# Stick-breaking attention summed by parts: scanned products times differences of neighbouring values

## The chip, the cores and the metric

The kernel runs on one core of one Trainium2 chip. The time is device microseconds from one launch to its end. The kernel before took 1382.73 us (median of three runs, 1382.43 to 1384.61).

## The reference, cut to what matters

The program is one decoder layer on 1024 tokens of width 1024: a mixer with two head groups (SSD and stick-breaking attention, eight heads of 64 each), cross-attention to 256 memory tokens, a squared-ReLU MLP, and norms. Only the stick-breaking attention is changed:

```python
def stick_breaking_attention(q, k, v):
    """q,k,v (B,H,S,Dh). A[t,s] = sigmoid(z_ts) * prod_{s<j<t} (1 - sigmoid(z_tj)), s < t strictly."""
    ...
    for i in range(s_len // Q_BLOCK):
        ...
        logits = jnp.einsum("bhqd,bhkd->bhqk", qb, kb) * scale
        ...
        log_stay = jnp.where(mask, jax.nn.log_sigmoid(-logits), 0.0)
        log_beta = jax.nn.log_sigmoid(logits)
        later = lax.cumsum(log_stay, axis=3, reverse=True) - log_stay
        w = jnp.where(mask, jnp.exp(log_beta + later), 0.0)
        outs.append(jnp.einsum("bhqk,bhkd->bhqd", w, vb))
```

For a row t, let R[s] be the product of the staying probabilities 1 - sigmoid(z) over s <= j < t, with R[t] = 1. The weight of position s is sigmoid(z_ts) R[s+1], which is also R[s+1] - R[s].

## The kernel before, in words

All float32 operands of a matmul are split into a high part (rounded by ScalarE) and a low part (the rest, by VectorE); a product is three matmuls (`mm3`), or two where one side's parts are stacked. The helper `split` (L104 and L107 in the profile: `act` and `tt`) makes both parts. `stt` is L114. The order of each engine's queue is fixed when the program is built: instructions go in the order in which they are traced, those under `later(by)` ahead (negative) or behind (positive), as far as their operands and buffers are expected to be there. `interleave` traces two streams side by side.

Early part, up to about 236 us: the input projections and the SSD heads. `proj_v(0)` makes the values of heads 0 to 3, `proj_qk(0)` and `proj_qk(1)` queries and keys of heads 0 to 3; they are traced beside `ssd`, which loads VectorE and ScalarE. `proj_v` takes eight token tiles of 128 in turn: 24 matmuls into a PSUM tile `vps` of 128 by 256 (`mm_ps`: three buffers `m0` and one `m1` in the early part; `qk_ps`: the three `m0` in the later one), ScalarE writes the high part into a tile `vst`, VectorE the low part, and SP's queue stores both to `vd` in DRAM (L573).

Attention, from about 250 to 516 us: eight heads, the first seven beside the rest of the projections (`proj_qk(2)`, `proj_v(1)`, `proj_qk(3)`, the memory's keys and values), the last beside the first part of the output projection. Per head the POOL queue loads values (`vt`), queries (`qs`) and keys (`kk`). Rows of queries go in eight blocks i of 128, with W = 128 (i + 1) columns. For each: matmuls `z` (L723); ScalarE's sigmoid of minus z into `stay` and of z into `beta` (L104); POOL sets one column behind the row to 0 (L717); VectorE scans `stay` from right to left (L727), so that it holds the products R; VectorE multiplies `beta` by `stay` shifted by one column (L107). Blocks go in pairs m; for a pair, TensorE transposes the rows of `beta` in 128 by 128 pieces (`wT`, L745), the result is split (`wTh` and `wTl`, `wlast` for the piece on the diagonal), and matmuls with the values sum into `ops` (L759). After every second pair the two halves of `ops` are added into `oT`. `beta` and `stay` have two narrow and two wide buffers each.

The scan runs with multiply and add, its second operand `dg1` being zeros with an identity in the last 128 columns, so that it starts at 1 on the diagonal:

```python
nc.vector.tensor_tensor_scan(out=stay[:, 0:W][:, ::-1], data0=stay[:, 0:W][:, ::-1],
                             data1=B.dg1[:, S - W:S][:, ::-1], initial=0.0,
                             op0=ALU.mult, op1=ALU.add)
tt(beta[:, 0:W], beta[:, 0:W], stay[:, 1:W + 1], ALU.mult)
```

Of the kernel before, what the change touches and what calls it, by code (L numbers as in the profile page):

```python
# [76 lines left out]
# columns of the packed per-partition constants  # L77
C_GMIX, C_GSSD, C_GSB, C_CW, C_CB, C_GMEM, C_GXA, NCOLS = 0, 8, 12, 16, 40, 46, 54, 62
# pieces of the packed weights, in the order of their use
# [11 lines left out]
def hybrid_trunk(ctx: ExitStack, tc: tile.TileContext, xT, x, cols, rows, gain, fing, wzd, wp, out):  # L91
# [39 lines left out]
    @contextmanager  # L131
    def later(by):
        """what is traced here gives way on its engine to what is traced up to `by` instructions after it"""
        tc.cur_priority += by
        yield
        tc.cur_priority -= by

# [10 lines left out]
                            fill=0.0, base=0, channel_multiplier=-1)  # L148
    nhalf = cp.tile([P, NT], F32, name="nhalf")
# [9 lines left out]
    # the first use of the scalar engine's functions, before any data is there  # L159
# [15 lines left out]
    def staging():  # L175
        """a tile that weights are loaded to: one in three from the pool of a phase that has room for it"""
        nst_[0] += 1
        if third and nst_[0] % 3 == 0:
            return third[0].tile([P, 528], F32, tag="wst3", bufs=1, name="wst")
        return wr.tile([P, 528], F32, tag="wst", bufs=2, name="wst")  # L180
# [26 lines left out]
    def wsl(ws, k, lo, n, width=256):  # L207
        """columns lo..lo+n of row block k in a chunk cut into pieces of several row blocks"""
        per = 512 // width if width != 264 else 2
        h, l = ws[k // per]  # L210
        o = (k % per) * width + lo
        return h[:, o:o + n], l[:, o:o + n]
# [11 lines left out]
    def interleave(a, b, total_a, total_b, need=None):  # L224
        """trace two streams side by side: each yields the share of its work that it has just traced;
        b may also yield ("need", x), which traces a up to x first"""
        da = db = 0.0
        a, b = iter(a), iter(b)
        live_a = live_b = True
        while live_a or live_b:  # L230
            if live_a and (not live_b or da / total_a <= db / total_b):
                v = next(a, None)
                live_a = v is not None
                da += v or 0.0
                continue
            v = next(b, None)
            if v is None:
                live_b = False
            elif isinstance(v, tuple):
                while live_a and da < v[1]:  # L240
                    w = next(a, None)
                    live_a = w is not None
                    da += w or 0.0
            else:
                db += v

    def rows_T(hn):
        """128 by 512 -> [128 columns, 4, 128 rows], in PSUM"""
# [6 lines left out]
    qd = dp.tile([8, P, S], F32, name="qd")  # L255
    kd = dp.tile([8, 192, S], F32, name="kd")
    vd = dp.tile([S, 8, P], F32, name="vd")
    rd = dp.tile([64, P], F32, name="rd")
# [6 lines left out]
    # =================== phase A: input projection and SSD ===================  # L265
# [23 lines left out]
    def load_x(k):  # L289
        """a block of xT: times the gain, split"""  # L290
# [19 lines left out]
    # the tensor engine's clock rises once it has been busy for some microseconds: products that nothing reads,  # L310
    # while the first loads are under way
# [26 lines left out]
    def conv_block(fb, ps2):  # L338
        """fb: 0..3 xs, 4 B, 5 C"""
# [37 lines left out]
    # factors of the stick-breaking logits' rows  # L377
    rq = [cp.tile([P, NT], F32, name=f"rq{i}") for i in range(2)]
    for r, f in zip(rq, (0.125, -0.125)):
        ts(r, rtok, f, None, ALU.mult)  # L380
# [12 lines left out]
    # token-major projections: z (with dt), v  # L393
# [32 lines left out]
    # a = -exp(a_log) = -sigmoid(a_log) / sigmoid(-a_log)  # L426
# [53 lines left out]
    def decay(c):  # L480
        """exp of minus the sums of a * dt between a chunk's tokens, 1 before the row's own"""
# [28 lines left out]
    def ssd():  # L510
      state = None
      for c in range(NT):
# [44 lines left out]
        # gate, sums of squares for the norm  # L557
# [6 lines left out]
    def proj_v(ch, p, ps_fn):  # L564
        ws = pieces(f"v{ch}", 0, 4)
        for t in range(NT):
            ps = tok_proj(ws, t, 256, 256, "vps", ps_fn)
            pv = ps[:, :256].rearrange("p (h d) -> p h d", h=4)
            vt = p.tile([P, 512], F32R, tag="qh", bufs=2, name="vst").rearrange("p (h c) -> p h c", h=4)
            with later(-EV):  # L570
                act(vt[:, :, 0:64], pv, scale=rtok[:, t:t + 1])
                stt(vt[:, :, 64:128], pv, rtok[:, t:t + 1], vt[:, :, 0:64].bitcast(F32), ALU.mult, ALU.subtract)
            nc.sync.dma_start(out=vd[t * P:(t + 1) * P, 4 * ch:4 * ch + 4, :], in_=vt.bitcast(F32))  # L573
            yield 1.0
# [77 lines left out]
    def need(h):  # L652
        """the share of the streams beside it that a head waits for"""
# [9 lines left out]
    # =================== phase B: stick-breaking attention ===================  # L663
    oT = big(1, [P, 4, S], F32, "oT")

    class Bufs:
        """the tiles that attention works in"""

        # narrow and wide rows: so many from the start, so many once the projection's operands are gone
        ROWS = {"beta": {True: 2, False: 2}, "stay": {True: 2, False: 2}}  # L670

        def __init__(self, ctx):
# [3 lines left out]
            nc.gpsimd.tensor_copy(out=self.dg1[:, S - P:S], in_=ident)  # L676
            self.wlast = [[p.tile([P, 512], F32R, name=f"wlast{a}{b}") for b in range(2)] for a in range(1)]
            for a in self.wlast:
                for b in a:
                    nc.gpsimd.memset(b[:, 256:384].bitcast(F32), 0.0)  # L680
# [15 lines left out]
    def attention(heads, B, need=lambda h: 0):  # L696
        for h in heads:
# [3 lines left out]
            nc.gpsimd.dma_start(out=vt, in_=vd.rearrange("(t p) h c -> p t (h c)", p=P)[:, :, P * h:P * h + P])  # L701
            qs = B.t("qs", [P, S], 2)
# [9 lines left out]
            for m in range(4):  # L712
                wb = []
                for i in (2 * m, 2 * m + 1):
                    W = P * (i + 1)
                    beta, stay = B.row("beta", W), B.row("stay", W)
                    nc.gpsimd.memset(stay[:, W:W + 1], 0.0)  # L717
                    for off in range(0, W, 512):
# [3 lines left out]
                        for a in range(2):  # L722
                            nc.tensor.matmul(out=z[:, 0:nn], lhsT=qs[:, i * P:(i + 1) * P],  # L723
                                             rhs=ks[a][off // 512][:, 0:nn], start=a == 0, stop=a == 1)
                        act(stay[:, off:off + n], z[:, 0:n], AF.Sigmoid, scale=rq[1][:, i:i + 1])
                        act(beta[:, off:off + n], z[:, 0:n], AF.Sigmoid, scale=rq[0][:, i:i + 1])
                    nc.vector.tensor_tensor_scan(out=stay[:, 0:W][:, ::-1], data0=stay[:, 0:W][:, ::-1],  # L727
                                                 data1=B.dg1[:, S - W:S][:, ::-1], initial=0.0,
                                                 op0=ALU.mult, op1=ALU.add)
                    tt(beta[:, 0:W], beta[:, 0:W], stay[:, 1:W + 1], ALU.mult)  # L730
                    wb.append(beta)
# [4 lines left out]
                for s2_ in range(m + 1):  # L736
# [19 lines left out]
                    for sb in range(2):  # L756
                        v = vt[:, 2 * s2_ + sb, :]
# [3 lines left out]
                if m % 2 == 1:  # L761
                    od = oT[64 * hh:64 * hh + 64, h // 2, 512 * (m // 2):512 * (m // 2) + 512]
                    act(od, ops[64:128, :])
                    tt(od, ops[0:64, :], od, ALU.add)
# [17 lines left out]
    def load_h(n, t, after=None):  # L782
        """not before `after` is written: what is needed sooner has the queues till then"""
# [13 lines left out]
    # output projection, by the heads of the first kind  # L797
# [44 lines left out]
    # =================== phase C: output projection, cross-attention ===================  # L842
# [30 lines left out]
    def turn(t):  # L873
        """rows of h, transposed and split"""
# [36 lines left out]
    # the row factors go into the softmax  # L911
# [18 lines left out]
    # softmax over the memory, values  # L930
# [49 lines left out]
    # the first half's normed rows are needed until its last projections: their places are taken after them  # L980
# [31 lines left out]
    # the products of the MLP go by blocks of two by two in seven products (Winograd's form):  # L1012
    # S1 = A21 + A22, S2 = S1 - A11, S3 = A11 - A21, S4 = A12 - S2
    # T1 = B12 - B11, T2 = B22 - T1, T3 = B22 - B12, T4 = T2 - B21
    # P1 = A11 B11, P2 = A12 B21, P3 = S4 B22, P4 = A22 T4, P5 = S1 T1, P6 = S2 T2, P7 = S3 T3
    # C11 = P1 + P2, U2 = P1 + P6, U3 = U2 + P7, C12 = U2 + P5 + P3, C21 = U3 - P4, C22 = U3 + P5
# [16 lines left out]
    def norm_rows(t):  # L1033
        """rows of h, normed: two tiles of 512 columns"""
# [20 lines left out]
    def normB(t):  # L1055
        """the normed rows, transposed: the right-hand operands of the first product, 128 tokens of them"""
# [49 lines left out]
    # =================== phase D: squared-ReLU MLP, final norm ===================  # L1106
    def prod(ps, a, b):
        """one of the seven products: a of two tiles [128, 4 * 128], b one of B"""
# [33 lines left out]
    # the left-hand operands of the second product's seven, in DRAM  # L1142
# [75 lines left out]
    def prod2(q, ops, accumulate, tail=False):  # L1218
        """a product of a group: four blocks of tokens, accumulated over the group's pairs"""
# [26 lines left out]
    def squares(t, c, n, st=None):  # L1246
        """sums of squares of half a row block"""
# [5 lines left out]
    def gained(t, c, n, eng, gfin):  # L1253
        """times the final gain: out of place, as the squares are of what comes in"""
# [19 lines left out]
    for g in range(NG):  # L1274
        Bm = []

        def load(j):
# [7 lines left out]
            # B11, B12, B21, B22  # L1285
# [56 lines left out]
def _layout(inp):  # L1342
# [5 lines left out]
    def cut(w, rows_per, n0, n1, k0=0, k1=None):  # L1348
        """columns n0..n1 of w: rows in blocks of 128, rows_per blocks side by side in a piece"""
# [53 lines left out]
```

## Time and profile before

| | us |
|---|---|
| median of three runs (lowest, highest) | 1382.73 (1382.43, 1384.61) |
| span of the profiled execution | 1381.4 |
| TensorE, VectorE, ScalarE busy in the span | 1318.0, 1002.7, 721.8 |
| of 141 to 236 us (95.0): TensorE, VectorE, ScalarE | 95.0, 66.2, 41.5 |
| of 236 to 516 us (280.0): TensorE, VectorE, ScalarE | 259.0, 237.1, 191.8 |

Of the profiled execution only the span is given, from its first to its last instruction; the median of the runs is 1.3 us above it. An engine's busy time is the time that its instructions cover. Matmuls are pipelined and their ends are modelled, so a busy TensorE need not be at its peak. PEld is the load of weights into TensorE, which overlaps matmuls. A wait is put down to what released it last. The granted TensorE clock has a mean of 0.992 of full speed over the span.

### The profile page before, as it was taken

The numbers are of one execution on the slowest core, as the hardware profiler recorded it, in microseconds if no ns is written. First come the engines' busy times: TensorE is split into PE (matmuls) and PEld (weight loads), VectorE is DVE, ScalarE is ACT, GpSimd is POOL, SyncE is SP. The second block draws the span as 40 slices with busy tenths as digits, with TensorE's granted clock in tenths as the row PEclk, the third lists the DMA queues.
The fourth block names the chain that finished last, engine by engine and source line by source line (L and its number), as shares of the span: only waits on it lengthen the run. The fifth ranks groups of instructions, "written<-read, shape, count | busy, mean of one in ns | idle before, by whom it ended". The sixth has DMA issues, their size and how long they took to land.

```text
span 1381.4 us, 18631 instructions
## 1 busy us (share of the span) xinstructions
PE 1318.0 (95%) x6469; PEld 1064.5 (77%) x6469; DVE 1002.7 (73%) x1570; ACT 721.8 (52%) x1384; POOL 234.8 (17%) x293
## 2 busy tenths in 40 slices
PE   9999999999988999999898999999999999999886
PEld 7989977787766778887676888888887888888765
DVE  7748864688999875638789666666559855677896
ACT  7355642667777653626555544554444544444343
POOL 0000002111101110000263323321331000000543
PEclk9999999999999999999998999999999999999999
DMA  6111355854567224111224445444368933633242
GB/s 215 39 62 49 125 157 137 229 145 138 142 196 204 70 79 127 47 31 31 92 77 151 163 156 163 134 141 153 130 210 297 317 112 93 234 92 98 71 127 86
DMA packets 102878, 183.79 MB, mean 133 GB/s; under 512 B 9664, under 2 KB 20992, under 8 KB 102784
## 3 DMA queue, kind: packets, MB, share of 16 engines
q1 hardware_dynamic: 85168, 158.14, 36.2%
q0 software_dynamic: 15664, 18.88, 5.4%
q10 hardware_dynamic: 1952, 5.58, 1.2%
q8 instruction: 51, 0.84, 0.2%
q14 instruction: 43, 0.35, 0.1%
HBM read 128.00 MB, written 54.56 MB: 132 GB/s over the span
## 4 chain that ended last, share of the span: by engine, by line
PE 74%; DVE 15%; ACT 4%; issue 3%; DMA 2%; POOL 1%; SPq 0%; DVEq 0%; POOLq 0%; ACTq 0%
PE P L203 7%; PE P L205 7%; PE P L204 7%; PE pr L203 6%; PE pr L204 6%; PE pr L205 6%; DVE stay L727 4%; DVE wlo L107 3%; PE qkps L203 2%; PE o L205 2%; PE qkps L204 2%; PE qkps L205 2%; PE o L204 2%; PE o L203 2%; PE ops L759 2%
## 5 line engine op out<-in xcount | busy, mean ns | idle before, releaser
L204 PE MATMUL pr<-wlo,whi 128*128 128x512 f32 x448 | 177.7, 397 | 10.9 <-DVE wlo L107 10.7
L203 PE MATMUL pr<-whi 128*128 128x512 f32 x448 | 176.8, 397 | 0.7 <-ACT whi L104 0.7
L205 PE MATMUL pr<-whi,wlo 128*128 128x512 f32 x448 | 177.2, 395 | 0.0
L107 POOL TENSOR_TENSOR c<-c 128x512 f32<-128x512 f32 x64 | 88.9, 1400 | 247.9 <-ACT c L104 224.3
L204 PEld LDWEIGHTS pr<-wlo,whi 128*128 128x128 f32 x448 | 84.4, 188 | 34.8 <-DVE wlo L107 15.3
L107 DVE TENSOR_TENSOR wlo<-w1r,whi 128x512 fp32r<-128x512 f32 x92 | 78.2, 851 | 41.8 <-ACT whi L104 41.5
L104 ACT ACTIVATE whi<-w1r 128x512 fp32r<-128x512 f32 x92 | 58.1, 632 | 94.6 <-PE P L204 70.0
L203 PE MATMUL P<-T,whi 128*128 128x512 f32 x256 | 101.7, 397 | 1.9 <-ACT T L104 1.9
L205 PE MATMUL P<-T,wlo 128*128 128x512 f32 x256 | 101.5, 396 | 0.0
L204 PE MATMUL P<-T,whi 128*128 128x512 f32 x256 | 101.1, 395 | 0.0
L203 PEld LDWEIGHTS pr<-whi 128*128 128x128 f32 x448 | 84.3, 188 | 21.3 <-ACT whi L104 1.4
L205 PEld LDWEIGHTS pr<-whi,wlo 128*128 128x128 f32 x448 | 84.4, 188 | 19.8
L104 ACT ACTIVATE c<-c 128x512 f32<-128x512 f32 x128 | 78.7, 628 | 26.1 <-DVE c L107 24.7
L727 DVE TENSOR_TENSOR_SCAN stay<-stay,dg 128x128 f32<-128x128 f32 (+3 forms) x64 | 85.0, 1346 | 6.6 <-ACT stay L104 6.2
L104 ACT ACTIVATE whi<-wst 128x512 fp32r<-128x512 f32 (+1 forms) x88 | 54.5, 628 | 58.6 <-PE o L205 16.6
L104 ACT ACTIVATE whi<-us 128x512 fp32r<-128x512 f32 x64 | 40.3, 629 | 83.0 <-PE pr L204 73.8
L203 PE MATMUL P<-B,whi 128*128 128x512 f32 x192 | 76.9, 401 | 0.0
L204 PE MATMUL P<-B,whi 128*128 128x512 f32 x192 | 76.6, 399 | 0.0
L205 PE MATMUL P<-B,wlo 128*128 128x512 f32 x192 | 76.5, 398 | 0.0
L107 DVE TENSOR_TENSOR wlo<-wst,whi 128x512 fp32r<-128x512 f32 (+1 forms) x88 | 61.1, 706 | 21.0 <-ACT whi L104 20.4
L107 DVE TENSOR_TENSOR wlo<-pair,whi 128x512 fp32r<-128x512 f32 x96 | 74.3, 774 | 0.0
L107 DVE TENSOR_TENSOR wlo<-us,whi 128x512 fp32r<-128x512 f32 x64 | 47.6, 744 | 36.3 <-ACT whi L104 36.0
(327 smaller groups left out, 3515.1 us busy)
## 6 DMA issues: line engine op xcount, KB each, us to landing
ud<-c SPq DMA_DIRECT2D x112, 256.0 KB, 2.7
wst<-in_wp SPq DMA_DIRECT2D x104, 256.0 KB, 2.8
w1r<-in_wp SPq DMA_DIRECT2D x16, 1024.0 KB, 6.4
us<-ud SPq DMA_DIRECT2D x64, 256.0 KB, 2.6
pair<-in_wp SPq DMA_DIRECT2D x16, 1024.0 KB, 6.7
kk<-kd POOLq DMA_DIRECT2D x32, 256.0 KB, 5.5
p<-ud SPq DMA_DIRECT2D x24, 256.0 KB, 2.6
u<-ud SPq DMA_DIRECT2D x24, 256.0 KB, 2.7
```

Of the source, the lines that this page charges most:

```text
L104: nc.scalar.activation(out=out, in_=in_, func=func, **kw)
L107: (eng or nc.vector).tensor_tensor(out=out, in0=a, in1=b, op=op)
L203: nc.tensor.matmul(out=ps, lhsT=a[0], rhs=b[0], start=start, stop=False)
L204: nc.tensor.matmul(out=ps, lhsT=a[0], rhs=b[1], start=False, stop=False)
L205: nc.tensor.matmul(out=ps, lhsT=a[1], rhs=b[0], start=False, stop=stop)
L727: nc.vector.tensor_tensor_scan(out=stay[:, 0:W][:, ::-1], data0=stay[:, 0:W][:, ::-1], data1=B.dg1[:, S - W:S][:, ::-1], initial=0.0, op0= ...
L759: nc.tensor.matmul(out=ops[:, oc:oc + 256], lhsT=v, rhs=w[:, sb * 256:sb * 256 + 256], start=(s2_ == 0 and sb == 0 and j == 0), stop=(last ...
```

## The change

Summed by parts, the output of a row t is v[t-1] minus the sum over s < t of R[s] (v[s] - v[s-1]), with v[-1] = 0. So the scanned products R go into the transposes and the matmuls directly, `beta` and its product are not formed, and `proj_v` stores differences of neighbouring values in place of values. From the diagonal on, R is 1: the scan takes the maximum with a triangle `tri` in place of adding an identity. The term v[t-1] comes out of the last block of a pair, where the weights to the right of the diagonal are 1: there a second set `vl` (stored in `ve`) is used, whose rows are the plain values less the neighbour (the last row without its own), and the sign is turned where `ops` is read.

Rows must be moved down by one partition to form the differences. `proj_v` collects two tiles in `vt`, and three transfers on SP's queue write the shifted copy `vb`: the last row of the pair before, the last row of the first tile, and 127 rows of both tiles at once. VectorE forms `vl` and `vb`, and three splits and three stores follow in place of two. The new tiles `vb` and `vl` share the tag `ql` (two buffers) with the low parts of `proj_qk`, the split results the tag `qh` (two buffers).

```diff
     def proj_v(ch, p, ps_fn):
         ws = pieces(f"v{ch}", 0, 4)
+        prev = None
         for t in range(NT):
             ps = tok_proj(ws, t, 256, 256, "vps", ps_fn)
-            pv = ps[:, :256].rearrange("p (h d) -> p h d", h=4)
-            vt = p.tile([P, 512], F32R, tag="qh", bufs=2, name="vst").rearrange("p (h c) -> p h c", h=4)
+            odd = t % 2
+            if not odd:
+                vt = p.tile([P, 2, 256], F32, tag="vv", bufs=2, name="vv")
             with later(-EV):
-                act(vt[:, :, 0:64], pv, scale=rtok[:, t:t + 1])
-                stt(vt[:, :, 64:128], pv, rtok[:, t:t + 1], vt[:, :, 0:64].bitcast(F32), ALU.mult, ALU.subtract)
-            nc.sync.dma_start(out=vd[t * P:(t + 1) * P, 4 * ch:4 * ch + 4, :], in_=vt.bitcast(F32))
+                act(vt[:, odd], ps[:, :256], scale=rtok[:, t:t + 1])
+            if odd:
+                vb = p.tile([P, 2, 256], F32, tag="ql", bufs=2, name="vb")
+                if prev is None:
+                    nc.gpsimd.memset(vb[0:1, 0], 0.0)
+                else:
+                    nc.sync.dma_start(out=vb[0:1, 0], in_=prev[P - 1:P, 1])
+                nc.sync.dma_start(out=vb[0:1, 1], in_=vt[P - 1:P, 0])
+                nc.sync.dma_start(out=vb[1:P], in_=vt[0:P - 1])
+                vl = p.tile([P, 512], F32, tag="ql", bufs=2, name="vl")[:, :256]
+                stt(vl, vt[:, 1], notlast, vb[:, 1], ALU.mult, ALU.subtract)
+                tt(vb, vt, vb, ALU.subtract)
+                for j, src in enumerate((vb[:, 0], vb[:, 1], vl)):
+                    o = p.tile([P, 4, P], F32R, tag="qh", bufs=2, name="vst")
+                    with later(-EV):
+                        split(o[:, :, 0:64], o[:, :, 64:128], src.rearrange("p (h d) -> p h d", h=4))
+                    dst = ve[t // 2] if j == 2 else vd[(t - 1 + j) * P:(t + j) * P]
+                    nc.sync.dma_start(out=dst[:, 4 * ch:4 * ch + 4, :], in_=o.bitcast(F32))
+                prev = vt
             yield 1.0
...
-        ROWS = {"beta": {True: 2, False: 2}, "stay": {True: 2, False: 2}}
+        ROWS = {"stay": {True: 2, False: 3}}
...
-            nc.gpsimd.tensor_copy(out=self.dg1[:, S - P:S], in_=ident)
+            nc.gpsimd.tensor_copy(out=self.dg1[:, S - P:S], in_=tri)
...
-                for b in a:
-                    nc.gpsimd.memset(b[:, 256:384].bitcast(F32), 0.0)
+                for b, v in zip(a, (1.0, 0.0)):
+                    nc.gpsimd.memset(b[:, 256:384].bitcast(F32), v)
...
+            vl = B.t("vl", [P, 4, P], 2)
+            nc.gpsimd.dma_start(out=vl, in_=ve.rearrange("t p h c -> p t (h c)")[:, :, P * h:P * h + P])
...
-                    beta, stay = B.row("beta", W), B.row("stay", W)
-                    nc.gpsimd.memset(stay[:, W:W + 1], 0.0)
+                    stay = B.row("stay", W)
...
-                        act(stay[:, off:off + n], z[:, 0:n], AF.Sigmoid, scale=rq[1][:, i:i + 1])
-                        act(beta[:, off:off + n], z[:, 0:n], AF.Sigmoid, scale=rq[0][:, i:i + 1])
+                        act(stay[:, off:off + n], z[:, 0:n], AF.Sigmoid, scale=rq[:, i:i + 1])
...
-                                                 op0=ALU.mult, op1=ALU.add)
-                    tt(beta[:, 0:W], beta[:, 0:W], stay[:, 1:W + 1], ALU.mult)
-                    wb.append(beta)
+                                                 op0=ALU.mult, op1=ALU.max)
+                    wb.append(stay)
...
-                        v = vt[:, 2 * s2_ + sb, :]
+                        v = vl[:, m, :] if last and sb == 1 else vt[:, 2 * s2_ + sb, :]
...
-                    act(od, ops[64:128, :])
-                    tt(od, ops[0:64, :], od, ALU.add)
+                    act(od, ops[64:128, :], scale=-1.0)
+                    tt(od, od, ops[0:64, :], ALU.subtract)
```

`notlast` is a column of ones with a 0 in the last row; `rq` keeps the factor -0.125 alone.

## Rows read from the trace of the kernel before

**Rows 1.** The page: span; each engine's busy time, share, instructions
```profile
span 1381.4 us, 18631 instructions
...
PE 1318.0 (95%) x6469; PEld 1064.5 (77%) x6469; DVE 1002.7 (73%) x1570; ACT 721.8 (52%) x1384; POOL 234.8 (17%) x293
```

**Rows 2.** Each engine's busy time in two stretches of the span
```profile
core 0: us, PE busy (x) PEld busy (x) DVE busy (x) ACT busy (x) POOL busy (x), PEclk, DMA share, GB/s
141.00:236.00 95.00, 95.00 (x546) 78.25 (x545) 66.20 (x123) 41.47 (x93) 3.10 (x4) 1.00 0.48 135
236.00:516.00 280.00, 258.96 (x1456) 203.54 (x1455) 237.06 (x350) 191.75 (x408) 40.96 (x132) 0.99 0.55 152
```

**Rows 3.** The chain that ended last, 236 to 516 us, shares by line
```profile
by line: DVE stay L727 21.2%; PE ops L759 7.7%; issue 7.4%; DVE beta L107 6.8%; DMA wst<-in_wp 5.0%; ACT stay L104 5.0%; PE wT L745 4.3%; DVE wTl L107 4.2%; ACT beta L104 4.2%; PE z L723 2.9%; ACT whi L104 2.7%; PE qkps L204 2.7%; PE qkps L
```

**Rows 4.** VectorE groups, 236 to 516 us: busy us, mean ns | idle before
```profile
L727 DVE TENSOR_TENSOR_SCAN stay<-stay,dg 128x128 f32<-128x128 f32 (+3 forms) x64 | 85.0, 1346 | 6.6 <-ACT stay L104 6.2
L107 DVE TENSOR_TENSOR beta<-beta,stay 128x128 f32<-128x128 f32 (+3 forms) x64 | 47.6, 750 | 9.4 <-PE z L723 5.4 <-ACT beta L104 2.3 <-POOL h L785 0.8
L107 DVE TENSOR_TENSOR wlo<-wst,whi 128x512 fp32r<-128x512 f32 x32 | 21.7, 685 | 6.0 <-ACT whi L104 5.7
```

**Rows 5.** ScalarE groups by shape, 236 to 516 us
```profile
L104 ACT ACTIVATE beta<-z,rq 128x512 f32<-128x512 f32 x48 | 33.3, 693 | 7.3 <-PE wT L745 7.1
L104 ACT ACTIVATE beta<-z,rq 128x384 f32<-128x384 f32 x16 | 9.3, 581 | 3.4 <-PE wT L745 3.4
L104 ACT ACTIVATE beta<-z,rq 128x256 f32<-128x256 f32 x16 | 7.6, 475 | 0.0
L104 ACT ACTIVATE beta<-z,rq 128x128 f32<-128x128 f32 x16 | 6.3, 393 | 0.0
```

**Rows 6.** Tile vst, 140 to 236 us: ns min/median/max, first and last start
```profile
L104 ACT ACTIVATE vst<-vps,rtok x8: 453/472/476, 145.0 to 173.0; 128x256 fp32r<-128x256 f32 x8
L114 DVE SCALAR_TENSOR_TENSOR vst<-vps,rtok,vst x8: 475/479/484, 145.8 to 173.7; 128x256 fp32r<-128x256 f32 x8
L573 SPq DMA_DIRECT2D vd<-vst x8: 319/320/407, 146.3 to 174.2; - x8
```

**Rows 7.** The same tile, 236 to 516 us
```profile
L104 ACT ACTIVATE vst<-vps,rtok x8: 467/477/497, 266.3 to 324.1; 128x256 fp32r<-128x256 f32 x8
```

**Rows 8.** Groups on tiles of 128x256 by shape, 236 to 516 us
```profile
L107 DVE TENSOR_TENSOR wlast<-wT,wlast 128x256 fp32r<-128x256 f32 x32 | 13.3, 415 | 1.0 <-ACT wlast L104 1.0
L104 ACT ACTIVATE wlast<-wT 128x256 fp32r<-128x256 f32 x32 | 12.2, 381 | 2.0 <-PE wT L745 2.0
```

**Rows 9.** DMA, whole run: packets, MB, share; issues, KB each, us to landing
```profile
q1 hardware_dynamic: 85168, 158.14, 36.2%
...
vd<-vst SPq DMA_DIRECT2D x16, 256.0 KB, 2.0
...
kd<-qh SPq DMA_DIRECT2D x32, 128.0 KB, 3.1
```

**Rows 10.** TensorE in order of time: start us, us; two short stretches
```profile
309.27 0.28 PE L203 MATMUL vps<-whi,xh 128*128 128x256 f32 x1
309.39 0.28 PE L204 MATMUL vps<-wlo,xh 128*128 128x256 f32 x1
...
354.05 0.39 PE L203 MATMUL qkps<-xh,whi 128*128 128x512 f32 x1
354.28 0.39 PE L204 MATMUL qkps<-xl,whi 128*128 128x512 f32 x1
```

**Rows 11.** Waits, 236 to 516 us: us in total, times, longest us
```profile
POOL stay L717 <- DVE beta L107: 125.0, 40, 8.7
POOL kk L710 <- PE z L723: 28.4, 7, 5.5
ACT beta L104 <- PE wT L745: 10.5, 10, 2.4
ACT whi L104 <- DMA wst<-in_wp: 9.9, 10, 3.3
```

More of the change, by code (lines that the diff above doesn't have):

```diff
@@ L148, in hybrid_trunk @@
                             fill=0.0, base=0, channel_multiplier=-1)
+    notlast = cp.tile([P, 1], F32, name="notlast")
+    nc.gpsimd.tensor_scalar(out=notlast, in0=ident[:, P - 1:P], scalar1=-1.0, scalar2=1.0, op0=ALU.mult, op1=ALU.add)
     nhalf = cp.tile([P, NT], F32, name="nhalf")
@@ L257, in hybrid_trunk @@
     vd = dp.tile([S, 8, P], F32, name="vd")
+    ve = dp.tile([4, P, 8, P], F32, name="ve")
     rd = dp.tile([64, P], F32, name="rd")
@@ L376, in hybrid_trunk @@
     rtok = rstd_of(cp, sps[:, :NT], NT, D, "rtok")
-    rq = [cp.tile([P, NT], F32, name=f"rq{i}") for i in range(2)]
-    for r, f in zip(rq, (0.125, -0.125)):
-        ts(r, rtok, f, None, ALU.mult)
+    rq = cp.tile([P, NT], F32, name="rq")
+    ts(rq, rtok, -0.125, None, ALU.mult)
     rbc = xp.tile([P, S], F32, name="rbc")
```

## The prediction, made before the change was run

> **What bounds the kernel now.** I read the page's first part, then the stretches, then the chain of waits inside the one that matters, then its costliest groups. TensorE is recorded busy for 95% of a span of 1381.4 us [rows 1]. The change touches only 141 to 516 us: the value projections of the early part (beside the SSD part) and the attention. From 141 to 236 us TensorE's records leave no idle time at all; from 236 to 516 us they leave 280.0 - 259.0 = 21 us, VectorE is busy 237 us of the 280 and ScalarE 192 [rows 2]. Matmul records overlap: neighbours start 0.12 us apart at 256 columns and 0.23 us at 512, while each is recorded as 0.28 and 0.39 us long [rows 10]. So recorded idle time is the least that TensorE has to spare, not the most. The chain through this stretch runs over VectorE more than over anything else: the scans hold 21.2%, the product `beta` 6.8%, the second sigmoid 4.2% [rows 3]. That is where the change cuts.
>
> **What goes.** The 64 products leave VectorE: 47.6 us [rows 4]. The 96 second sigmoids leave ScalarE: 33.3 + 9.3 + 7.6 + 6.3 = 56.5 us [rows 5]. The 64 one-column memsets leave the POOL queue, where they stood 125.0 us waiting for products, with the loads of keys behind them [rows 11]; I book nothing for that, because those loads then wait for their buffers (28.4 us in the same rows) and no matmul is named as waiting for one. Of the chain the removed steps hold 6.8 + 4.2 = 11.0% of 280 us = 31 us. The least that they give back is less than TensorE's idle 21 us, if another wait is next. What is late next is the scan, which stays, and the buffers: a row is now held through its transposes, as `beta` was (ScalarE waited 10.5 us for that [rows 11]), with three wide buffers in place of two and two. I take the middle of 21 and 31: **26 us saved**, with 10 and 31 as ends.
>
> **What stays at the same price.** The scan's second operation becomes a maximum and its second operand a triangle. No row shows a scan with a maximum; the nearest is the scan itself, 1346 ns in the mean [rows 4], and I take that. A scan that got one more pass would cost at most the removed products again, 47.6 us; nothing speaks for it. The transposes, splits, value matmuls and the two operations on `oT` keep their number and shapes. One more load per head (256 KB, eight in all) goes to the POOL queue that has lost its memsets. The change of `rq`, the constant `notlast` and the fills of `wlast` are single small instructions: nothing.
>
> **What is added.** For each pair of token tiles in `proj_v`, four pairs in each of two projections: three transfers from SBUF to SBUF that move the rows down by one, on SP's queue; one scalar_tensor_tensor; one subtraction of 128x512; three splits where there were two; three stores where there were two. In engine time this is little. VectorE per pair: 0.48 + 0.69 + 3 x 0.42 less 2 x 0.48 = 1.5 us; ScalarE one 0.47 us evacuation kept per tile plus 3 x 0.38 = 1.1 us more [rows 4, 6, 8]. Over four pairs that is 6 us and 5 us beside work that leaves 29 us of VectorE idle early and, after the removal, some 85 us idle later: nothing on the path.
>
> **The shift is the doubtful price.** It moves 127 rows of 2 KB (254 KB) and everything else of the pair waits for it. From below: the store of `vst`, 128 rows and 256 KB, lands in 2.0 us [rows 9]. From above: all 127 rows one after the other. SP's queue moved 85168 packets in 36.2% of 16 engines' 1381.4 us, which is 94 ns a packet [rows 9]; 127 of them take 11.9 us. Of the store's 2.0 us its eight packets an engine are 0.75, so 1.25 is fixed; together **13.2 us**. Every listed transfer has 64 or 128 rows, and 16 equal shares exist for them; 127 rows have no equal shares but single rows. I take the upper end, and keep the lower as a rival.
>
> The Trainium skill, DMA: Bandwidth & Descriptors, section "Why a DMA increments its semaphore by 16 and not by 1", says that a transfer gets the largest number of engines up to 16 that divides the outermost count on both sides, and names 127 partitions as a case that gets one. No run here shows it. By that rule the shift has the upper price and the sum below; by the nearest row, 2.0 us, the sum would be the second rival's.
>
> **What waits for it.** `vb` and `vl` take turns in two buffers of one tag (`ql`), so a pair's shift can't start before the pair ahead is split. A pair then takes 13.2 + 0.6 of issue (two single-row transfers go ahead of it at 0.32 each [rows 6]) + 0.48 + 0.69 + about 1.8 for the overlapped splits = 16.8 us. VectorE, ScalarE and SP each work in a fixed order, so behind the waiting subtraction stand the SSD part's VectorE work (early) and the scans and splits of attention (later); behind the waiting stores on SP stand the next weight pieces.
>
> Early projection: its eight evacuations start from 145.0 to 173.0 us, 4 us a tile [rows 6]. With the first pair complete at about 149.5, four pairs in file end at 149.5 + 4 x 16.8 = 216.7, where the last store now starts at 174.2: 42 us late. TensorE can run ahead by the four PSUM tiles that `mm_ps` has: 4 x 24 matmuls x 0.23 = 22 us [rows 10]. So **20 us lost**, with 5 (other work fits in between) and 42 as ends. TensorE has no idle time here to take it up [rows 2].
>
> Later projection: evacuations from 266.3 to 324.1 us, 16.5 us a pair [rows 7], which is nearly the serial pace already, so no queue builds up. What remains is four waits of 13.2 - 2.0 = 11.2 us on VectorE and ScalarE. TensorE can run ahead by three PSUM tiles of 24 x 0.12 = 2.9 us, 8.6 us at best, so between 4 x 2.6 = 10 and 45 us; I take **20 us lost**, nearer to the covered end, since the attention's own matmuls also go on for a while. The lower end is 0, if VectorE's new 85 us of idle time happen to lie there.
>
> **Sum.** 1381.4 - 26 + 20 + 20 = 1395.4 us for the profiled execution. Only its span is given; the median of the runs, 1382.73, is 1.3 above it, so **1397 us**. The case's own range is 1384 to 1422 (relief 21 with losses of 30 and 30 at the top).
>
> **Rivals.**
> First, the shift is slow and hidden: the subtraction stands late enough in VectorE's and ScalarE's order that other work fills the 13 us, and only the buffers cost something. For it: VectorE loses 47.6 us of work; the later pace is the serial one [rows 7]. Against it: TensorE has no spare time from 141 to 236 us. 1381.4 - 26 + 8 + 4 + 1.3 = 1369 us.
> Second, the shift is spread over the engines like the store of `vst` [rows 9]: it lands in 2 to 4 us and a pair takes under 8 us, its pace of today. For it: the nearest row. Against it: 127 rows. Then 1381.4 - 26 + 1.3 = 1357 us.
> Third, no change: the scan with its held buffers takes the place of the product, so the relief is 10 us, and a half-hidden shift gives 11 back: 1383 us. For it: the scans hold three times the product's share of the chain [rows 3].
> The first two end on the other side from the forecast, and the point at which the sign turns is clear: losses in `proj_v` of 26 us in all, 3.3 us for each of eight shifts.
>
> **Chances.** Forecast 0.50, first rival 0.26, second 0.14, third 0.10. The sizes are rough, so some of each case spills over. Faster by over 0.2%: 0.06 of the forecast, 0.20 of the first, all 0.14 of the second, 0.02 of the third = 0.42. Within 0.2% (2.8 us, about what a measurement of this kernel can tell from no change): 0.04 + 0.03 + 0.04 = 0.11. Slower: 0.40 + 0.03 + 0.04 = 0.47. Cases of both signs hold much of the chance, so the range has to reach from the second rival, 1357, to the top of the forecast's, 1422.
>
> **What would show it.** In the profile after: the median time to landing of `vb` from `vt` near 13 us (forecast, first rival) or near 2 (second). The evacuations of the early projection ending near 200 us in place of 173, and TensorE idle between 150 and 236 us where it had none, with VectorE's subtraction named behind a transfer. The stretch that holds attention, 280 us now [rows 2], being shorter by some 26 us would show the relief, with `beta` gone and VectorE near 195 us busy in it. The prediction is wrong if the shift lands in a few microseconds, if TensorE stays gapless through the early stretch, or if the relief is far above 31 us, which would say that TensorE's hidden reserve (overlapped records [rows 10]) was the larger part.

## The result, and the profile after

| | us |
|---|---|
| before, median of four runs beside the changed kernel | 1383.65 |
| after, median of four runs (lowest, highest) | 1467.91 (1465.84, 1471.80) |
| after / before, 95% interval | 1.0606 [1.0585, 1.0627] |
| span of the profiled execution after | 1467.2 |

The change made the kernel 84 us slower, 46 us above the top of the predicted range. The first lines of the page after answer to [rows 1]. In its second part each digit is the busy share of one of 40 slices of 36.7 us; PEclk is the granted clock in tenths.

```profile
span 1467.2 us, 18461 instructions
...
PE 1331.6 (91%) x6469; PEld 1078.6 (74%) x6469; DVE 973.1 (66%) x1529; ACT 686.3 (47%) x1312; POOL 237.4 (16%) x240
...
PE   8999757996459989999988899999999999999987
...
PEclk9999878998869999999999899999999999999999
```

In all VectorE lost 30 us and ScalarE 35.5 us of work, and TensorE has the same number of matmuls. TensorE has two dips that it didn't have before, around the fifth to seventh and the tenth to twelfth slice: those are the two runs of `proj_v`. The stretches that answer to [rows 2] hold about the same matmuls, so they are longer here (busy time of each engine, granted clock); the last two rows are 20 us from inside each dip.

```profile
core 0: us, PE busy (x) PEld busy (x) DVE busy (x) ACT busy (x) POOL busy (x), PEclk, DMA share, GB/s
141.00:282.00 141.00, 108.51 (x554) 87.31 (x553) 70.45 (x135) 44.85 (x106) 5.79 (x9) 0.85 0.37 109
282.00:600.00 318.00, 256.32 (x1436) 206.07 (x1435) 201.15 (x297) 153.68 (x326) 38.96 (x73) 0.92 0.55 151
...
200.00:220.00 20.00, 11.20 (x40) 8.65 (x41) 6.03 (x12) 1.77 (x4) 0.00 (x0) 0.66 0.34 106
...
420.00:440.00 20.00, 9.94 (x42) 7.83 (x42) 6.24 (x15) 4.49 (x12) 0.92 (x1) 0.68 0.31 101
```

The early stretch went from 95 us without a gap to 141 us with 32 us of idle TensorE, the later one from 280 to 318 us with 62 us idle. What stops TensorE is in the waits of 141 to 600 us (us in total, times, longest):

```profile
DVE vl L114 <- DMA vb<-vv: 85.0, 8, 12.8
...
ACT vst L104 <- DVE vb L107: 50.5, 4, 15.4
...
PEld wT L769 <- DVE stay L752: 32.3, 35, 13.8
...
PE yp L538 <- DVE seg L107: 25.8, 3, 10.7
PE wT L769 <- DVE stay L752: 25.7, 26, 13.6
...
PEld yp L538 <- DVE seg L107: 20.0, 2, 11.2
PE ops L783 <- DVE wlast L107: 19.9, 2, 10.1
...
PE ops L783 <- DVE wTl L107: 10.4, 2, 10.2
```

Read from top to bottom it is one story: eight times VectorE waits for the shifted copy, 10.6 us each; ScalarE's splits wait for VectorE; and TensorE waits for things that have nothing to do with `proj_v` (SSD's `seg`, attention's `stay`), because VectorE makes them after the instruction on which it stands. Of TensorE's 94 us of idle time in the two stretches, 82 end with something of VectorE's (the four lines of PE: 25.8 + 25.7 + 19.9 + 10.4). In order of time (start, length; in brackets the idle time before and its releaser):

```profile
151.46 0.72 SPq L588 DMA_DIRECT2D vb<-vv  x1
...
154.61 0.68 DVE L107 TENSOR_TENSOR wb<-xstok,rowt 128x512 f32<-128x512 f32 x1
165.09 0.48 DVE L114 SCALAR_TENSOR_TENSOR vl<-vv,notlast,vb 128x256 f32<-128x256 f32 x1 [9.79 <-DMA vb<-vv]
...
169.82 1.97 PE L538 MATMUL yp<-wa,seg 128*128 128x64 f32 x8 [8.61 <-DVE seg L107]
...
351.37 0.58 PE L783 MATMUL ops<-wTl,vt 128*128 128x256 f32 x1 [10.23 <-DVE wTl L107]
```

The first shift is issued at 151.46 us and used at 165.09: 13.6 us. The eight take 13.6 to 17.7 us, 14.7 in the mean. VectorE stops at 155.3 us (154.61 + 0.68), TensorE at 161.2 (169.82 - 8.61): it ran ahead by 5.9 us, not 22, then stood for 8.6 us before `yp`, SSD's matmul on a product that VectorE had yet to make. The later projection shows the same with attention's `ops`.

The list of DMAs, answering to [rows 9] (KB each, median us to landing; the first line has no median):

```profile
vd<-vst SPq DMA_DIRECT2D x16, 256.0 KB, 2.3
...
vb<-vv SPq DMA_DIRECT2D x8, 254.0 KB
vb<-vv SPq DMA_DIRECT2D x14, 1.0 KB, 1.9
```

127 rows took at least 13.6 us from issue to use where 128 rows of the same size, stored to DRAM, land in 2.3. From 153 to 164 us the first shift is all that moves, and the DMA list of these 11 us has one queue (packets, MB, share of 16 engines):

```profile
q1 hardware_dynamic: 120, 0.25, 6.5%
```

That is a packet of 2 KB every 92 ns and the busy time of one engine in sixteen (6.5% x 16 = 1.04): the rows go in single file. The scan with a maximum costs what the scan with an addition cost in [rows 4], 1348 against 1346 ns in the mean (VectorE groups, 282 to 600 us):

```profile
L752 DVE TENSOR_TENSOR_SCAN stay<-stay,dg 128x128 f32<-128x128 f32 (+3 forms) x64 | 85.2, 1348 | 12.2 <-ACT stay L104 11.9
```

### The profile page after: what moved, and what is told of

It is laid out like the page before. It is cut to its first block, busy times and chain, and to the rows that moved or that the text cites. A ratio compares the mean times of both kernels' runs of the same rounds, so it can differ in the third digit from the quotient of the medians.

```text
span 1467.2 us, 18461 instructions
## 1 busy us (share of the span) xinstructions
PE 1331.6 (91%) x6469; PEld 1078.6 (74%) x6469; DVE 973.1 (66%) x1529; ACT 686.3 (47%) x1312; POOL 237.4 (16%) x240
## 4 chain that ended last, share of the span: by engine, by line
PE 51%; DVE 7%; ACT 2%; issue 2%; DMA 2%; POOL 1%; POOLq 0%; DVEq 0%; ACTq 0%
PE P L206 7%; PE P L208 7%; PE P L207 7%; PE pr L206 6%; PE pr L207 6%; PE pr L208 6%; DVE wlo L107 2%; PE o L208 2%; PE o L206 2%; PE o L207 2%; DMA wst<-in_wp 1%; PE xqps L206 1%; PE xqps L208 1%; PE xqps L207 1%; DVE stay L752 1%
## 5 line engine op out<-in xcount | busy, mean ns | idle before, releaser
L752 DVE TENSOR_TENSOR_SCAN stay<-stay,dg 128x128 f32<-128x128 f32 (+3 forms) x64 | 85.2, 1348 | 12.2 <-ACT stay L104 11.9
L769 PE MATMUL wT<-ident,stay 128*128 128x128 f32 x288 | 51.9, 284 | 26.5 <-DVE stay L752 25.7
```

The lines of the kernel that those rows point to most:

```text
L769: nc.tensor.transpose(out=t4[:, o:o + P], in_=wb[ii][:, b * P:(b + 1) * P], identity=ident)
```

## Experiments

Two questions: is the single-file transfer the whole loss, and by which way does it reach the end; and what is the attention's half of the change worth without it?

**1. The shift in two pieces, 112 rows and 15.** Nothing else differs from the changed kernel.

```diff
-                nc.sync.dma_start(out=vb[1:P], in_=vt[0:P - 1])
+                nc.sync.dma_start(out=vb[1:113], in_=vt[0:112])
+                nc.sync.dma_start(out=vb[113:P], in_=vt[112:P - 1])
```

> The 127-row shift goes as two transfers of 112 and 15 rows; nothing else differs from the changed kernel. Theory A (127 rows move in single file, 13 us from issue to use, and VectorE and ScalarE stand in order behind it): the shift is there 2 to 4 us after its issue, VectorE's waits for vb fall from 85 us to under 20, TensorE is without gaps again from 141 to 236 us, and the time is 1355 to 1375 us. Theory B (the chain through two shared buffers with three transfers and three splits is the cost, whatever a transfer takes): above 1430 us. Theory C (the loss is in the new attention): above 1430 us with VectorE's waits for vb gone.

Measured: 1375.56 us, 0.9937 [0.9922, 0.9952] of before. Cutting the transfer in two took 92 us off (1467.9 - 1375.6) and turned the loss into a gain. The DMA list of this kernel, and its stretches:

```profile
vb<-vv SPq DMA_DIRECT2D x8, 224.0 KB, 3.6
...
vb<-vv SPq DMA_DIRECT2D x8, 30.0 KB, 2.7
```

```profile
141.00:236.00 95.00, 94.50 (x538) 77.14 (x537) 69.85 (x134) 44.22 (x104) 3.23 (x5) 1.00 0.53 157
236.00:506.00 270.00, 250.95 (x1443) 200.61 (x1442) 200.31 (x296) 152.31 (x324) 41.18 (x77) 1.00 0.65 180
```

112 rows, 7.5 times the bytes, land little later than 15. Against these rows the loss of the changed kernel can be taken apart, since both hold the same matmuls: of 141 + 318 - 95 - 270 = 94 us, TensorE's idle time is 75 (32.5 + 61.7 less 0.5 + 19.1) and longer busy time of its matmuls is 19 (108.5 + 256.3 less 94.5 + 251.0), at granted clocks of 0.85 and 0.92 where this kernel has 1.00 in both. VectorE's wait for `vb` fell from 85.0 us to 1.0, and TensorE's longest wait for the scans from 13.8 us to 1.1:

```profile
PEld wT L770 <- DVE stay L753: 21.7, 38, 1.1
...
PE wT L770 <- DVE stay L753: 14.1, 30, 0.9
```

**2. The same 127 rows from the POOL queue.** The second kernel of experiment 5 and the first two of experiment 8 have this edit too:

```diff
-                nc.sync.dma_start(out=vb[1:P], in_=vt[0:P - 1])
+                nc.gpsimd.dma_start(out=vb[1:P], in_=vt[0:P - 1])
```

> The same 127-row shift issued from the POOL queue. If the row count alone makes the single file: about 13 us from issue to use again, and 1440 us or more. If it is the way in which SP's queue divides a transfer: 3 to 6 us, and 1360 to 1385 us.

Measured once: 1373.58 us; the DMA list shows what the queue does with the same 127 rows.

```profile
vb<-vv POOLq DMA_DIRECT2D x8, 254.0 KB, 3.1
```

Timed again beside a run of the kernel before:

> The shift on the POOL queue once more, timed in five rounds: 1372 to 1376 us, a ratio of 0.990 to 0.996 to the kernel before.

Measured: 1374.72 us, 0.9923 [0.9910, 0.9935]. So it is not the number 127 and not the bytes but 127 rows on SP's queue. This version computes all that the reference asks and is 0.8% faster than before, like the split of experiment 1 (1375.6).

**3. Which of the two projections costs what.** The first projection keeps the single-file shift, the second is split as in experiment 1.

```diff
-                nc.sync.dma_start(out=vb[1:P], in_=vt[0:P - 1])
+                if ch == 0:
+                    nc.sync.dma_start(out=vb[1:P], in_=vt[0:P - 1])
+                else:
+                    nc.sync.dma_start(out=vb[1:113], in_=vt[0:112])
+                    nc.sync.dma_start(out=vb[113:P], in_=vt[112:P - 1])
```

> The changed kernel with the shift in one transfer of 127 rows in the early projection alone; in the later one it goes as 112 and 15 rows. It parts the 92 us between the changed kernel and the split one. Theory A1 (the early part has no idle TensorE time, so it holds the loss that the trace shows there, 44 to 46 us): 1415 to 1425 us, and some 46 us left for the later projection. Theory A2 (most of the loss is in the attention, where scans and sigmoids stand behind the shift): under 1405 us.

Measured: 1417.48 us, 1.0236 [1.0219, 1.0253]. The four early shifts cost 1417.5 - 1375.6 = 42 us, the four later ones 1467.9 - 1417.5 = 50 us. The stretches agree: the early one is long at a low clock, the attention is nearly as in experiment 1.

```profile
141.00:290.00 149.00, 116.94 (x589) 94.16 (x588) 71.71 (x137) 45.89 (x106) 10.11 (x15) 0.86 0.41 117
290.00:556.00 266.00, 247.49 (x1423) 197.79 (x1421) 204.31 (x302) 156.33 (x331) 35.10 (x67) 0.99 0.63 176
```

**4. A single-file transfer that nobody waits for.** The kernel before, with a store of 127 rows per pair to a place that is never read.

```diff
+    vx = dp.tile([8, P, 512], F32, name="vx")
...
             nc.sync.dma_start(out=vd[t * P:(t + 1) * P, 4 * ch:4 * ch + 4, :], in_=vt.bitcast(F32))
+            if t % 2:
+                nc.sync.dma_start(out=vx[4 * ch + t // 2, 1:P], in_=vt.rearrange("p h c -> p (h c)")[0:P - 1].bitcast(F32))
```

> The kernel before with one more transfer for each pair of value tiles: 127 rows of 2 KB of the stored tile to DRAM on SP's queue, eight in all, which nothing waits for except the tile's next use. Theory A: the cost is in the engines that wait, so under 10 us is lost (1383 to 1393). Theory D (the single file blocks the queue for the weight pieces and stores behind it): 1410 us or more. The tile is held 11 us longer, which can stop ScalarE's next evacuation; that loss would show as ScalarE's wait for a transfer, and count as theory A's.

Measured: 1414.51 us, 1.0217 [1.0201, 1.0233], 29.5 us more than before (1385.03, the median beside it). The time is where theory D had put it, and the theory that only a reader's wait costs much (under 10 us here) missed; but the largest wait is the one on the tile that the expectation had named. The waits (141 to 600 us) and the DMA list show where it goes:

```profile
ACT vst L104 <- DMA vx<-vst: 39.1, 5, 14.0
...
DVE vst L114 <- ACT vst L104: 26.8, 7, 9.4
```

```profile
vd<-vst SPq DMA_DIRECT2D x16, 256.0 KB, 6.6
```

The transfer holds its source tile, of which there are two, so the tile's next writer on ScalarE waits instead of a reader; and the ordinary stores of `vd` on the same queue now land in 6.6 us in the median in place of 2.0 [rows 9]. So a slow transfer can cost through its reader, through its source's next writer, and perhaps through transfers behind it: that those are late is shown, that it costs time is not. What each is worth in the changed kernel was not separated.

**5. The wait moved later in the program.** The differences of a pair are traced after the next pair's shift, with the single-file transfer on SP's queue and, in a second kernel, on POOL's.

```diff
+        def differences(t, vt, vb):
+            tt(vb, vt, vb, ALU.subtract)
...
+                if pend is not None:
+                    differences(*pend)
+                pend = (t, vt, vb)
```

> The single-file shift on SP's queue stays, but the differences of a pair are traced after the next pair of tiles, so that VectorE and ScalarE have other work ahead of them in their order (the second set is formed from the differences, in the place of the first half of the pair's tile). Theory A with the order as its lever: 1385 to 1425 us, since a pair still needs some 12 us of the file against the 7 us in which the early part makes one. If the order is no lever and the file alone counts: 1455 us or more.

Measured: 1468.47 us, 1.0598 [1.0584, 1.0613]: a miss. The waits (141 to 600 us) say why.

```profile
ACT vst L104 <- DVE vb L107: 93.0, 8, 14.4
...
DVE vb L107 <- DMA vb<-vv: 86.5, 8, 13.2
```

VectorE still waits eight times for 86.5 us. Tracing the subtraction later did not put VectorE's work ahead of it: the first wait begins right behind the same product `wb` as in the changed kernel, at 154.7 us in place of 155.3. So this does not tell whether a subtraction that stood 13 us later would be free.

> The deferred differences with the shift on the POOL queue. Nothing waits for the shift in the run with the POOL queue any more, so theory A expects no change: 1371 to 1377 us.

Measured: 1380.30 us, 0.9964 [0.9951, 0.9978], 5.6 us worse than the same shift without the deferral (1374.72), where no change was expected. With nothing left to hide, the deferral only costs; by which wait was not followed up.

**6. The attention's half alone.** The old `proj_v` is kept, and the last block of a pair takes its values from `vd` in the same shapes.

```diff
-            nc.gpsimd.dma_start(out=vl, in_=ve.rearrange("t p h c -> p t (h c)")[:, :, P * h:P * h + P])
+            nc.gpsimd.dma_start(out=vl, in_=vd.rearrange("(t p) h c -> p t (h c)", p=P)[:, 1::2, P * h:P * h + P])
```

> The new attention with the value projection of the kernel before: the values are stored as they are, the second set is read from every second tile of them, so the output is not the reference's; each instruction of the new attention is there. Theories A and B: the attention is relieved by 10 to 31 us, 26 at best guess, so 1352 to 1373 us, with the early part as before. Theory C: 1400 us or more.

Measured: 1375.18 us, 0.9934 [0.9918, 0.9951]. Taking 47.6 us of VectorE's and 56.5 us of ScalarE's work away, and the memsets, brings 10 us (1385.03 - 1375.18); which of them brings it was not separated. And since experiments 1 and 2 come to the same time, the new `proj_v` costs nothing that can be measured once its shift is quick.

**7. More buffers.** Experiment 6 with four wide rows in place of three.

```diff
-        ROWS = {"stay": {True: 2, False: 3}}
+        ROWS = {"stay": {True: 2, False: 4}}
```

> The new attention with the old value projection (1375.2 us), with four wide buffers for stay in place of three, so that the sigmoid of a pair's second row need not wait for the transposes of the row before. Theory H (rows held through their transposes hold back the relief): 1365 us or less. Theories S and P: 1372 to 1377 us.

Measured: 1375.06 us, 0.9931 [0.9916, 0.9945]. No change against 1375.18: the number of wide buffers is not what keeps the relief small.

**8. What bounds the attention after the relief.** From experiment 2, once the scans are left out, once the matmuls with the low part of the weights (160 of them); and those matmuls left out of the kernel before.

```diff
-                    nc.vector.tensor_tensor_scan(out=stay[:, 0:W][:, ::-1], data0=stay[:, 0:W][:, ::-1],
-                                                 data1=B.dg1[:, S - W:S][:, ::-1], initial=0.0,
-                                                 op0=ALU.mult, op1=ALU.max)
```

> The kernel with the shift on the POOL queue (1373.6 us) with the 64 scans left out: the sigmoids go to the transposes as they are, so the output is not the reference's. It takes 85 us from VectorE. Why was the relief 10 us and not 26? Theory S (the scan has taken the product's place in the chain): 15 us or more are saved, 1358 us or less. Theory P (TensorE in its fixed order, with its own matmuls, is the limit by now): 1364 to 1372 us.

Measured: 1358.27 us, 0.9811 [0.9797, 0.9826]: 16 us less than 1374.72 for 85 us of VectorE's work. By the expectation's own bounds (15 us or more) that speaks for theory S, the scan in the product's place.

```diff
-                        for j, w in enumerate((wh, wl)):
+                        for j, w in enumerate((wh,)):
```

> The kernel with the shift on the POOL queue (1373.6 us) without the matmuls of the weights' low parts: 160 matmuls of 256 columns fewer, about 19 us of TensorE at 0.12 us each; the splits are still made, so the low part of the weights is left out of the result. Theory P: 14 to 19 us are saved, 1354 to 1360 us. Theory S: TensorE waits in their place, 1366 to 1373 us.

Measured: 1355.58 us, 0.9791 [0.9776, 0.9805]: 19 us less than 1374.72, which is all of the 160 x 0.12 = 19 us that these matmuls take at the spacing of [rows 10], and speaks for theory P. (By the ratios to the kernel before, 0.9791 and 0.9923, it is 18 us.)

> The kernel before without the matmuls of the weights' low parts (160 of 256 columns fewer, about 19 us of TensorE), so the low part of the weights is left out of the result here too. If TensorE's own matmuls already bounded the attention of the kernel before: 14 us or more are saved, 1370 us or less, and the relief of VectorE could only ever bring what TensorE waits. If VectorE's scan and product bounded it: under 8 us are saved, 1376 us or more.

Measured: 1381.36 us, 0.9972 [0.9961, 0.9983]: the same matmuls were worth only 4 us (1385.31 - 1381.36, the median beside it) before the change. The stretch of attention in these three kernels, in the order scans left out, low part left out, low part left out of before:

```profile
236.00:488.00 252.00, 244.88 (x1441) 201.26 (x1440) 124.10 (x235) 152.68 (x327) 42.68 (x79) 1.00 0.70 194
```

```profile
236.00:490.00 254.00, 234.66 (x1293) 182.25 (x1293) 201.79 (x301) 155.74 (x329) 43.28 (x80) 1.00 0.70 193
```

```profile
236.00:516.00 280.00, 248.40 (x1303) 193.36 (x1302) 239.35 (x352) 194.57 (x411) 41.22 (x132) 0.96 0.54 152
```

In the last one TensorE has 32 us of idle time in 280 and little comes of it: VectorE is busy for 239 us, as before. After the change VectorE has 201 of 270 us, and 19 us of matmuls count in full. So TensorE's own matmuls, which hardly counted before, have become the nearer bound. Two things are left open. In the last kernel the granted clock of the stretch is 0.96 against 0.99 in [rows 2], which can have eaten a part of its gain; and that the 10 us are the whole distance between the two bounds is argued, not measured. Without the scans the stretch is 16 us shorter with TensorE busy to 97%; with them TensorE stands before its transposes for a row here and there (waits of 236 to 510 us in the version of experiment 2, timed):

```profile
PEld wT L769 <- DVE stay L752: 21.1, 38, 1.2
...
PE wT L769 <- DVE stay L752: 13.4, 29, 0.8
```

38 short waits, none over 1.2 us; without the scans TensorE's idle time in the stretch is 7 us (252 - 244.9) in place of 18. That a single scan's length decides these waits, and not VectorE's total load, is a reading, not a test.

## Why the prediction was right and wrong

**The shift's price: right, a little low.** 13.2 us was forecast from the packets of [rows 9], one row after the other; 13.6 to 17.7 were seen, with 92 ns a packet where the forecast had 94, and one engine's worth of busy time. The rule of the Trainium skill, DMA: Bandwidth & Descriptors, section "Why a DMA increments its semaphore by 16 and not by 1", agrees: by it 127 partitions go to one engine on SP's queue, 112 to 16 and 15 to 15 (experiment 1: 3.6 and 2.7 us), and it names as an exception that the POOL queue spreads some direct copies of 127 partitions (experiment 2: 3.1 us). The nearest row, the store of 128 rows, was far from the case, and the choice of the upper end was the right one.

**The loss by the shift: right in kind, half in size.** 20 us early and 20 us later were forecast; experiment 3 gives 42 and 50. The steps that failed are "TensorE can run ahead by the four PSUM tiles that `mm_ps` has: 4 x 24 matmuls x 0.23 = 22 us" and its counterpart of "8.6 us at best" for each later wait. Two things are wrong with the first. Its spacing is that of 512 columns; the `vps` matmuls have 256, at 0.12 us in [rows 10], so four tiles hold 11.5 us. And free PSUM tiles are no licence to run ahead: TensorE's order is fixed as well, and among the `vps` matmuls stand SSD's and attention's, which need VectorE. It stopped 5.9 us after VectorE did, and at the first later shift 2.8 us after (341.1 and 338.4 us). The prediction named the work behind the waiting subtraction on VectorE, and did not go on to ask which matmuls wait for that work. Its own ends for full exposure, 42 and 45 us, were close to 42 and 50; with these ends and the lower relief of 10 the sum would have been 1460 us, but the top of the range, 1422, was made with losses of 30 and 30. That the early end is met to the microsecond is luck: it came from a pace that was too short, and the last store of the early projection is issued at 231.4 us, not 216.7.

The pace forecast for a pair, 16.8 us, came out at 19.8 (uses of the early shifts at 165.1 and 224.5 us, three pairs between): 14.7 us of shift, where 13.2 was forecast, and 5.2 from its use to the issue of the next, where the forecast had 3.6.

**The clock was not priced at all.** Of the 94 us that experiment 1 takes off the two stretches, 19 are longer busy time of matmuls in stretches where TensorE had stood idle; some of it can be records that overlap less behind a gap. Eight `yp` matmuls took 1.97 us right behind the wait of 8.61 us, above, at a granted clock of 0.50 (169.8 to 171.8 us); in the kernel before, at a granted clock of 1.00 and without such a wait, eight of the same kind took half:

```profile
163.84 1.00 PE L535 MATMUL yp<-wa,seg 128*128 128x64 f32 x8
```

A factor of two is that between TensorE's two levels, 1.2 and 2.4 GHz. So what a wait costs is more than its length. How much of the 19 us would have been hidden in other waits was not measured.

**The relief: too large.** "I take the middle of 21 and 31" gave 26 us; experiments 6 and 2 measure 10 and 11, the lower end kept for the range. The step that failed is reading the saving off the removed steps' share of the chain. The chain shows what ended last as things were; close behind it stood TensorE's own matmuls, as experiment 8 shows, and the scans. The prediction had even written that TensorE's recorded idle time, 21 us, is the least it has to spare. It was hardly to be had: of those 21 us, 18 remained after the change (269 less 250.9 busy in the version of experiment 2), as short waits for the scans.

**The rivals.** The first (slow but hidden) fell with experiment 3. The second (a quick shift) was wrong for this kernel, and describes experiments 1 and 2 in all but the size of the relief: 1357 forecast, 1375 measured. The third had the relief right at 10 us, for reasons that hold by half: a fourth wide buffer changed nothing (experiment 7), but the scan that it put in the product's place is worth 16 us (experiment 8). Its half-hidden shift was wrong.

**What was booked at nothing**: the subtraction, the third split and store, the `vl` loads, the maximum in the scan. Experiments 1, 2 and 6 agree within 1 us, so the first two, which experiment 6 lacks, were nothing; the scans took 85.2 us in place of 85.0; the `vl` loads are in all three kernels and were not tested. With the measured terms the sum is 1383.7 - 10 + 42 + 50 = 1466 us, against 1467.9; it has to come out so, since the terms are differences between these same kernels.

## What to carry to other kernels

Look at the row count of every transfer, not only at its bytes: a copy that moves rows down by one has 127, and on SP's queue here that meant single file; two pieces, or the POOL queue, cost one line and were worth 92 us. When an instruction gets a new wait, follow it through two engines: what stands behind it, and which matmuls need that; in queues of fixed order a wait on one can become a wait on all unless something independent is next everywhere. And before you book a relief from the chain, ask which engine comes next and how far behind it is: leaving some of that engine's work out, before and after, gives a good sign of it (4 us against 19 here).

## What was not expected of the hardware

Eight transfers of 127 rows that nobody reads cost 29.5 us in all, with waits of 39.1 us for the tile that they hold and with ordinary stores of the same queue landing in 6.6 us in place of 2.0. The granted clock fell to between 0.66 and 0.83 in the four stretches of 20 us from 160 to 240 us, in which TensorE was made to stand for up to 10.7 us at a time. And the POOL queue moved the same 127 rows in 3.1 us that took SP's queue 13.6 or more.
